# Three-branch attention in one kernel: heads stepped in pairs, other lags, banks and buffers

## The chip, the cores and the metric

The kernel runs on one core of a Trainium2 chip. The core has five engines with instruction queues of their own: TensorE (PE, matrix products; its weight loads are shown as PEld), VectorE (DVE), ScalarE (ACT), GpSimd (POOL) and SyncE (SP, which here only issues DMAs). They share an on-chip memory (SBUF) of 128 partitions, and PE writes its results to eight accumulation banks (PSUM) of 128 x 512 fp32 numbers. The metric is device time in microseconds of the whole program, one launch.

## The reference, cut to what matters

The program is a chain of blocks on 512 tokens of width 1024: a mixer, a cross attention, a gated MLP, a stick-breaking attention, an MLP, the three-branch attention that the change touches, and a last MLP. Of the three-branch attention:

```python
# 16 heads of 64, 4 groups of 4 heads share keys and values; 512 tokens
sc    = einsum(q, k_cmp) * scale            # 31 compressed blocks per group
p_cmp = softmax(where(valid_c, sc, NEG))
o_cmp = einsum(p_cmp, v_cmp)
...
ss    = einsum(q_rot, k_sel) * scale        # 8 blocks of 64: with top 16 of 8, all causal keys
o_sel = einsum(softmax(where(valid_s, ss, NEG)), v_sel)
...
sw    = einsum(q_rot, k_w) * scale          # window of 512: all causal keys again
o_win = einsum(softmax(where(valid_w, sw, NEG)), v_w)
...
out   = einsum(gates, stack([o_cmp, o_sel, o_win]))   # sigmoid gates per token, branch, head
return out @ w_o
```

`q_rot` is the query with a partial rotation. Since the sequence is 512 long, the selected and the window branch are both plain causal attention, each with keys and values of its own; the kernel computes them with the same code, as branch b = 0 and b = 1.

## The kernel before, in words

Every block splits fp32 operands into a high and a low part, and PE multiplies high by high, low by high and high by low. The program is written in a fixed order: each engine executes its instructions in the order in which the Python code emits them, and waits on semaphores where it needs another engine's result. A tile from a pool (`tmp`) with `bufs=n` is reused after n allocations of its tag, and the first writer waits for the last reader of the old content. PSUM banks come from lists by tag (`BANKS`) in rotation, with the same wait.

`n_attend` is the stage in question. It builds a list of steps and loops over them. Each group of four heads has one compressed step (`c_` functions, all four heads at once) and then, for each pair of heads and each branch b, the two heads one after the other, each with four steps: the four chunks of 128 queries in the order `QORD` = 3, 2, 0, 1. Chunk c sees 128(c+1) keys, so its tiles are 512, 384, 128 and 256 wide. That is 33 steps a group and 132 in all. In iteration i, the parts of different steps are emitted with lags, in the order of `ORDER`: the scores of step i (PE, bank `s`), the value products of step i-9 (PE, bank `av`), mask, scaling by -1/8 and row minimum of step i-1 (`n_bias`, DVE, L2065, into a tile `np`), the transpositions of step i-6 (PE, L2087, bank `t`), the exponential with row sum of step i-2 (ACT, L2070), the reciprocal of the sum of step i-3 (DVE, L2074), the scaling by reciprocal and gate of step i-4 (POOL, L2079), the split of a finished pair (`n_head`, ACT L548 and DVE L549), the move of step i-7 from bank `t` into the probability tile `pt` (`n_move`, ACT L2100 for chunks 3 and 0, DVE L2098 for 2 and 1), and last one call of each running generator (`tick`). The value products of a pair and a branch are emitted together once both heads' four chunks are moved: eight products for 64 + 64 output rows, before them, in branch 0, the compressed term.

`g_query(p)` rotates the queries of pair p, in twelve calls: a shuffle on DVE (L2031); six elementwise operations on POOL (L2034, L2036, L2038, twice); then for each of the two heads the high part on ACT (L2044), the low part on DVE (L2046) and a DMA from SP (L2049) that copies both to the other 64 partitions. In the trace each call's instruction stands behind what its engine was given in that iteration. The generator for the next pair starts in step 4 and step 20 of a group and makes one call a step.

Behind the steps, the output projection (`no0` to `no7`) starts with three banks that take the pairs' K blocks (`out(k)`) as they are ready, while the last steps drain.

Of the kernel before, what the change touches and what calls it, by code (L numbers as in the profile page):

```python
# [18 lines left out]
P = 128  # L19
T = 512  # L20
# [11 lines left out]
         "s": [0, 1, 2], "t": [3, 4, 5, 6], "av": [7], "f": [0, 1, 2, 3]}  # L32
NP = 8
# [433 lines left out]
class Kernel:  # L467
# [954 lines left out]
    def fetch(self, upto):  # L1422
        while self.fetched <= min(upto, KT - 1):
            m = self.fetched
            t = self.tmp(self.back_tag[0], bufs=self.back_tag[1])
# [316 lines left out]
    def _nsa(self):  # L1742
# [13 lines left out]
        self.heads = {}  # L1756
# [198 lines left out]
    def gate(self, gt):  # L1955
# [3 lines left out]
        for c in range(4):  # L1959
# [12 lines left out]
    ORDER = (("scores", 0), ("out", 9), ("bias", 1), ("turn", 6), ("exp", 2), ("sums", 3),  # L1972
             ("scale", 4), ("head", 10), ("move", 7), ("tick", 0))
    DRAIN, QSTART = 10, 4

    def n_attend(self):
        self.causal = self.wide("causal", self.ph, "causal")
        steps = []
        for g in range(4):
            steps.append(dict(g=g, c=3))  # L1980
            for h0 in (4 * g, 4 * g + 2):
                for b in range(2):
                    for h in (h0, h0 + 1):
                        for c in self.QORD:
                            steps.append(dict(g=g, h=h, b=b, c=c))
# [10 lines left out]
        for i in range(n + max(lag for _, lag in self.ORDER) + 1):  # L1996
            if i == n:
                lead = [(self.W.get(f"no{m}", 3 - m), self.bank("s")) for m in range(3)]
            for part, lag in self.ORDER:
                if part == "tick":  # L2000
                    self.tick()
                elif 0 <= i - lag < n:
                    u = steps[i - lag]
                    f = getattr(self, ("n_" if "h" in u else "c_") + part, None)
                    if f:
                        f(u)
            if i < n and i % 33 % 16 == self.QSTART and i < 116:
                self.bg.append(self.g_query(i // 33 * 2 + i % 33 // 16 + 1))
            j = i - n - self.DRAIN + 7
            if 0 < j < 8:  # L2010
                out(j - 1)
        nxt, nx = self.next_norm() if self.nxt else None, self.newx() if self.nxt else None
        self.back, self.fetched, self.back_tag = {}, 0, ("np", NP)
# [46 lines left out]
    def n_bias(self, u):  # L2060

        w = P * u["c"] + P
        p = u["p"] = self.tmp("np", bufs=NP)[:, :w]
        u["mx"] = self.tmp("nmx", (P, 1), bufs=8)
# [3 lines left out]
    def n_exp(self, u):  # L2068
        u["sm"] = self.tmp("nsm", (P, 1), bufs=8)
# [3 lines left out]
    def n_sums(self, u):  # L2073
        self.nc.vector.reciprocal(u["sm"], u["sm"])  # L2074
# [15 lines left out]
    def n_move(self, u):  # L2090
        h, b, c = u["h"], u["b"], u["c"]
        if c == self.QORD[0]:
            self.pt[h, b] = self.pt0 if self.npt % 3 == 2 else self.tmp("pt", (P, 13, P), bufs=2)
# [8 lines left out]
    def n_out(self, u):  # L2102
# [5 lines left out]
        if b == 0:  # L2108
            self.av = self.bank("av")
            cp, vc = self.cp  # L2110
            for e in range(2):
                self.mm(self.av[halves[e]], vc[:, (h - 1 + e) % 4, :], cp, True, False)
        pt = [self.pt.pop((h - 1 + e, b)) for e in range(2)]
# [100 lines left out]
```

## Time and profile before

| | |
|---|---|
| median of 3 runs | 2194.77 us (2191.74 to 2198.05) |
| the profiled execution | 2190.76 us |
| its span, first to last instruction | 2187.8 us |
| mean granted TensorE clock | 0.994 of full speed |
| PE busy | 2126.4 us (97%) |
| DVE, ACT, POOL busy | 1218.1, 885.0, 203.2 us |
| scores of the stage, first to last | 1611.57 to 1770.4 us |

Busy time is the time in which an engine had at least one instruction running; matmuls are pipelined, so a busy PE is not PE at its peak. An instruction's start to the next one's start on the same engine is what it occupies, often less than its duration. The stage is about 8% of the span.

### The profile page before, as it was taken

What the parts mean: (1) busy time and instruction counts of PE and PEld (TensorE: products, weight loads), DVE (VectorE), ACT (ScalarE), POOL (GpSimd) and SP (SyncE); (2) the same over time, 40 slices, a digit from 0 to 9 for tenths busy, and PEclk for the clock granted to TensorE, in tenths of its full rate; (3) what the DMA queues carried; (4) which work ended last, traced back from release to release, by engine and by line L of the source; (5) the groups of instructions that cost most, each with busy time, mean ns of one, the idle gap of its engine ahead of it and who ended that gap; (6) DMA issues with size and microseconds to landing.
All of it is one profiled execution on the core that took longest, in us unless ns stands there. A gap on an engine that the chain in (4) does not pass through costs nothing.

```text
span 2187.8 us, 26618 instructions
## 1 busy us (share of the span) xinstructions
PE 2126.4 (97%) x10250; PEld 1728.4 (79%) x10250; DVE 1218.1 (56%) x2052; ACT 885.0 (40%) x1457; POOL 203.2 (9%) x277
## 2 busy tenths in 40 slices
PE   8999999999999999999999999999988899999998
PEld 6788898888888888777688888888766668888886
DVE  5988665654443435566555343456667755534434
ACT  4533543433222224355435232234646744423322
POOL 1000000000000000122100000001047720000000
PEclk9999999999999999999999999999999999999999
DMA  4212444222333323422143233333421023333231
GB/s 148 73 63 78 160 129 135 68 78 87 97 98 97 99 80 110 133 62 75 49 135 97 97 96 97 97 100 123 138 83 31 21 73 102 106 97 98 95 100 64
DMA packets 63375, 205.93 MB, mean 94 GB/s; under 512 B 7952, under 2 KB 8336, under 8 KB 63120
## 3 DMA queue, kind: packets, MB, share of 16 engines
q1 hardware_dynamic: 59504, 196.86, 28.5%
q10 hardware_dynamic: 3744, 7.37, 0.9%
q8 instruction: 80, 1.31, 0.2%
q14 instruction: 47, 0.39, 0.1%
HBM read 189.39 MB, written 6.29 MB: 89 GB/s over the span
## 4 chain that ended last, share of the span: by engine, by line
PE 83%; DVE 7%; ACT 4%; POOL 3%; issue 2%; DMA 1%; ACTq 0%; POOLq 0%; SPq 0%; DVEq 0%
PE psum L539 63%; PE b L539 18%; POOL sph L1680 1%; ACT sT L1662 1%; ACT sT L1663 1%; PE psum L2087 1%; DVE spl L1685 1%; DVE wl L350 1%; DVE np L2065 1%; DVE sT L1657 1%; DMA nq<-nq 1%; DVE t L906 0%; DVE sT L1656 0%; POOL np L2079 0%; DVE st L1608 0%
## 5 line engine op out<-in xcount | busy, mean ns | idle before, releaser
L539 PE MATMUL psum<-xh,wh 128*128 128x512 f32 x1560 | 610.2, 391 | 1.5 <-DVE h L627 0.9
L539 PE MATMUL psum<-xh,wl 128*128 128x512 f32 x1560 | 607.5, 389 | 1.5 <-DVE wl L350 1.4
L539 PE MATMUL psum<-xl,wh 128*128 128x512 f32 x1560 | 607.4, 389 | 0.0
L341 ACT ACTIVATE wh<-ws 128x1024 fp32r<-128x1024 f32 (+1 forms) x346 | 356.9, 1039 | 372.6 <-PE psum L539 315.9
L350 DVE TENSOR_TENSOR wl<-ws,wh 128x1024 fp32r<-128x1024 f32 (+1 forms) x346 | 417.2, 1212 | 97.9 <-ACT wh L341 97.8
L539 PEld LDWEIGHTS psum<-xh,wl 128*128 128x128 f32 x1560 | 292.4, 187 | 64.4 <-DVE wl L350 2.8
L539 PEld LDWEIGHTS psum<-xh,wh 128*128 128x128 f32 x1560 | 292.5, 188 | 63.7 <-issue 2.3
L539 PEld LDWEIGHTS psum<-xl,wh 128*128 128x128 f32 x1560 | 292.5, 188 | 60.3
L539 PE MATMUL b<-xh,wh 128*128 128x512 f32 (+1 forms) x488 | 194.3, 398 | 6.6 <-ACT wh L341 6.6
L539 PE MATMUL b<-xh,wl 128*128 128x512 f32 (+1 forms) x488 | 192.2, 394 | 0.7 <-DVE wl L350 0.7
L539 PE MATMUL b<-xl,wh 128*128 128x512 f32 (+1 forms) x488 | 191.8, 393 | 0.0
L539 PE MATMUL psum<-hh,wh 128*128 128x512 f32 x320 | 125.0, 391 | 0.0
L539 PE MATMUL psum<-hh,wl 128*128 128x512 f32 x320 | 124.6, 389 | 0.0
L539 PE MATMUL psum<-hl,wh 128*128 128x512 f32 x320 | 124.5, 389 | 0.0
L1351 DVE TENSOR_TENSOR h<-h,psum 128x512 f32<-128x512 f32 x48 | 33.0, 688 | 161.2 <-PE psum L539 161.2
L1342 ACT ACTIVATE t<-t 128x512 f32<-128x512 f32 x64 | 40.5, 632 | 188.0 <-DVE t L1341 188.0
L539 PEld LDWEIGHTS b<-xh,wh 128*128 128x128 f32 (+1 forms) x488 | 92.0, 188 | 26.2 <-ACT wh L341 6.8
L539 PEld LDWEIGHTS b<-xh,wl 128*128 128x128 f32 (+1 forms) x488 | 91.7, 188 | 23.4 <-DVE wl L350 2.6
L539 PEld LDWEIGHTS b<-xl,wh 128*128 128x128 f32 (+1 forms) x488 | 92.1, 189 | 19.8 <-DVE xl L552 0.8
L539 PE MATMUL psum<-ks,nq 128*128 128x256 f32 (+2 forms) x256 | 72.5, 376 | 16.4 <-DVE nmx L2065 9.5
L1341 DVE SCALAR_TENSOR_TENSOR t<-psum,r_mlp 128x512 f32<-128x512 f32 x64 | 44.1, 689 | 79.2 <-PE psum L539 79.1
L2079 POOL TENSOR_SCALAR np<-np,nsm,gates 128x512 f32<-128x512 f32 (+3 forms) x128 | 81.2, 640 | 39.8 <-PE psum L2087 17.4
(485 smaller groups left out, 2873.0 us busy)
## 6 DMA issues: line engine op xcount, KB each, us to landing
ws<-in_wst SPq DMA_DIRECT2D x332, 512.0 KB, 3.4
h<-in_xT SPq DMA_DIRECT2D x16, 256.0 KB, 3.7
kk<-kk SPq DMA_DIRECT2D x16, 256.0 KB, 3.6
nq<-nq SPq DMA_DIRECT2D x16, 256.0 KB, 2.9
ws<-in_wst SPq DMA_DIRECT2D x8, 384.0 KB, 3.0
spill<-back SPq DMA_DIRECT2D x8, 256.0 KB, 2.0
back<-spill ACTq DMA_DIRECT2D x8, 256.0 KB, 3.5
spill<-h ACTq DMA_DIRECT2D x8, 256.0 KB, 5.7
```

The lines of the kernel that those rows point to most:

```text
L341: self.nc.scalar.activation(hi[:, :n], s, AF.Copy)
L350: e.tensor_tensor(lo[:, :n], s, hi[:, :n].bitcast(F32), op=ALU.subtract)
L539: self.nc.tensor.matmul(ps, a, b, start=start, stop=stop, skip_group_check=again)
L1341: nc.vector.scalar_tensor_tensor(t, ps, 0.0, norm.bc, op0=ALU.max, op1=ALU.mult)
L1342: nc.scalar.activation(t, t, AF.Square)
L1351: nc.vector.tensor_tensor(self.h[:, m, :], self.h[:, m, :], ps, op=ALU.add)
L1657: self.nc.vector.tensor_scalar(tb, zb[:, :, :384], 30.0, None, op0=ALU.min)
L1662: self.nc.scalar.activation(t, t, AF.Exp)
L1663: self.nc.scalar.activation(t, t, AF.Ln, bias=1.0)
L1680: self.nc.gpsimd.tensor_scalar(hi, t, 1.0, 0.0, op0=ALU.mult, op1=ALU.add)
L1685: self.nc.vector.tensor_tensor(lo, t, hi.bitcast(F32), op=ALU.subtract)
L2079: self.nc.gpsimd.tensor_scalar(u["p"], u["p"], u.pop("sm"), self.gates[:, u["c"], e:e + 1], op0=ALU.mult, op1=ALU.mult)
```

## The change

Both heads of a pair now share a step: a step scores, masks, scales, transposes and moves both heads' chunk c. A group has 17 steps, the stage 68. The lags are new (in steps of two heads): move 5, transpositions 4, value products 6, mask 1, exponential 1, reciprocal 2, scaling 2, split 9, and the move now comes right behind the scores. One reciprocal serves both heads. The value products go into a list of pieces (`todo`: compressed term, key chunk 0, key chunk 1, key chunks 2 and 3), and each step takes one. `tick` makes two calls a step, and the query generators start behind steps 1 and 9 of a group. The `s` tag has four banks instead of three, `t` three instead of four. The masked scores have a tag for each width with 2, 2, 2 and 3 buffers instead of eight shared ones of full width; `pt` has three buffers instead of two (a fourth, `pt0`, lies in another tile). The compressed branch's value tile `vc` is cleared and loaded five steps later and has one buffer. The residual tiles behind the stage are fetched into `pt` buffers, and the first blocks of the output projection are emitted in the seven iterations right behind the last scores.

```diff
 BANKS = {"b": range(8), "bp": [0], "bo": [1], "za": [2, 3], "zb": [4, 6],
-         "s": [0, 1, 2], "t": [3, 4, 5, 6], "av": [7], "f": [0, 1, 2, 3]}
-NP = 8
+         "s": [0, 1, 2, 3], "t": [4, 5, 6], "av": [7], "f": [0, 1, 2, 3]}
+NP = {0: 2, 1: 2, 2: 2, 3: 3}
...
-    ORDER = (("scores", 0), ("out", 9), ("bias", 1), ("turn", 6), ("exp", 2), ("sums", 3),
-             ("scale", 4), ("head", 10), ("move", 7), ("tick", 0))
-    DRAIN, QSTART = 10, 4
+    ORDER = (("scores", 0), ("move", 5), ("turn", 4), ("out", 6), ("av", 0), ("bias", 1),
+             ("exp", 1), ("sums", 2), ("scale", 2), ("head", 9), ("tick", 0))
...
         for g in range(4):
-            steps.append(dict(g=g, c=3))
+            steps.append((dict(g=g, c=3),))
             for h0 in (4 * g, 4 * g + 2):
                 for b in range(2):
-                    for h in (h0, h0 + 1):
-                        for c in self.QORD:
-                            steps.append(dict(g=g, h=h, b=b, c=c))
+                    for c in self.QORD:
+                        two = dict(g=g, h=h0, b=b, c=c), dict(g=g, h=h0 + 1, b=b, c=c)
+                        two[0]["two"] = two[1]["two"] = two
+                        steps.append(two)
...
                 if part == "tick":
-                    self.tick()
+                    self.tick(2)
+                elif part == "av":
+                    if self.todo:
+                        self.todo.popleft()()
                 elif 0 <= i - lag < n:
-                    u = steps[i - lag]
-                    f = getattr(self, ("n_" if "h" in u else "c_") + part, None)
-                    if f:
-                        f(u)
-            if i < n and i % 33 % 16 == self.QSTART and i < 116:
-                self.bg.append(self.g_query(i // 33 * 2 + i % 33 // 16 + 1))
-            j = i - n - self.DRAIN + 7
-            if 0 < j < 8:
-                out(j - 1)
+                    for u in steps[i - lag]:
+                        f = getattr(self, ("n_" if "h" in u else "c_") + part, None)
+                        if f:
+                            f(u)
+            if i % 17 in (1, 9) and i < n - 8:
+                self.bg.append(self.g_query(i // 17 * 2 + i % 17 // 8 + 1))
+            if 0 <= i - n < 7:
+                out(i - n)
...
-        self.back, self.fetched, self.back_tag = {}, 0, ("np", NP)
+        self.back, self.fetched, self.back_tag = {}, 0, ("pt", 3, (P, 13, P))
...
-        p = u["p"] = self.tmp("np", bufs=NP)[:, :w]
-        u["mx"] = self.tmp("nmx", (P, 1), bufs=8)
+        p = u["p"] = self.tmp(f"np{u['c']}", (P, w), bufs=NP[u["c"]])
+        u["mx"] = self.tmp("nmx", (P, 1), bufs=4)
...
     def n_sums(self, u):
-        self.nc.vector.reciprocal(u["sm"], u["sm"])
+        if u["h"] % 2:
+            self.nc.vector.reciprocal(u["sms"], u["sms"])
...
-            self.pt[h, b] = self.pt0 if self.npt % 3 == 2 else self.tmp("pt", (P, 13, P), bufs=2)
+            self.pt[h, b] = self.pt0 if self.npt % 4 == 3 else self.tmp("pt", (P, 13, P), bufs=3)
...
-            cp, vc = self.cp
+        av, (cp, vc) = self.av, self.cp
+        pt = [self.pt.pop((h - 1 + e, b)) for e in range(2)]
+
+        def first():
             for e in range(2):
-                self.mm(self.av[halves[e]], vc[:, (h - 1 + e) % 4, :], cp, True, False)
-        pt = [self.pt.pop((h - 1 + e, b)) for e in range(2)]
-        for j in range(4):
-            for e in range(2):
-                self.mm(self.av[halves[e], P * j:], self.vs[:, b, j, g, :],
-                        pt[e][:, 4 * j:3 * j + 4, :].rearrange("p c q -> p (c q)"),
-                        False, b == 1 and j == 3)
+                self.mm(av[halves[e]], vc[:, (h - 1 + e) % 4, :], cp, True, False)
+
+        def part(js):
+            for j in js:
+                for e in range(2):
+                    self.mm(av[halves[e], P * j:], self.vs[:, b, j, g, :],
+                            pt[e][:, 4 * j:3 * j + 4, :].rearrange("p c q -> p (c q)"),
+                            False, b == 1 and j == 3)
+
+        if b == 0:
+            self.todo.append(first)
+        for js in ((0,), (1,), (2, 3)):
+            self.todo.append(lambda js=js: part(js))
...
     def c_move(self, u):
-        cp = self.tmp("cp", bufs=1)
-        self.nc.scalar.activation(cp, u.pop("ps"), AF.Copy)
-        u["cp"] = cp, u.pop("vc")
+        nc, g = self.nc, u["g"]
+        cp, vc = self.tmp("cp", bufs=1), self.tmp("vc", (P, 4, 64), bufs=1)
+        nc.scalar.activation(cp, u.pop("ps"), AF.Copy)
+        nc.gpsimd.memset(vc, 0.0)
+        for h in range(4):
+            nc.sync.dma_start(out=vc[32 * h:32 * h + 32, h, :],
+                              in_=self.vcs[32 * g:32 * g + 32, :])
+        u["cp"] = cp, vc
```

## Rows read from the trace of the kernel before

**Rows 1.** The page: busy time and share of each engine, instructions.

```profile
PE 2126.4 (97%) x10250; PEld 1728.4 (79%) x10250; DVE 1218.1 (56%) x2052; ACT 885.0 (40%) x1457; POOL 203.2 (9%) x277
```

**Rows 2.** Windows: busy us (count) of PE, PEld, DVE, ACT, POOL, clock, DMA.

```profile
1611.57:1631.14 19.57, 13.68 (x63) 10.19 (x64) 14.93 (x59) 12.93 (x38) 12.80 (x19) 0.83 0.16 40
1631.14:1672.23 41.09, 36.04 (x237) 24.85 (x237) 32.10 (x130) 28.87 (x89) 29.72 (x47) 1.00 0.12 28
...
1754.72:1770.40 15.68, 15.68 (x107) 11.14 (x108) 10.82 (x54) 10.82 (x37) 8.98 (x15) 1.00 0.08 18
1770.40:1788.66 18.26, 17.77 (x97) 12.06 (x95) 6.16 (x17) 4.81 (x14) 3.96 (x6) 1.00 0.23 70
```

**Rows 3.** Chain of waits in the stage: start, us, what.

```profile
1663.50 0.47 PE psum L539 x2
...
1664.88 0.45 PE psum L2087 x4
...
1667.28 1.33 POOL np L2079 x2
...
1669.20 2.89 DMA nq<-nq
1672.23 3.87 PE psum L539 x22
...
1698.94 1.06 POOL np L2172
```

**Rows 4.** Timeline of PE: start us, busy us, line, operation, count.

```profile
1648.84 1.95 PE L539 MATMUL psum<-kb,h 128*128 128x128 f32 x16
1650.72 1.08 PE L539 MATMUL psum<-cp,vc 128*64 128x512 f32 x4
1651.63 0.59 PE L539 MATMUL psum<-pt,vs 128*64 128x512 f32 x1
...
1653.88 0.33 PE L2087 MATMUL psum<-small,np 128*128 128x128 f32 x1
```

**Rows 5.** Timeline of POOL, from the compressed branch's scaling.

```profile
1657.88 1.05 POOL L2172 TENSOR_TENSOR np<-np,csm 128x512 f32<-128x512 f32 x1 [1.55 <-DVE csm L2167]
1658.91 1.41 POOL L2079 TENSOR_SCALAR np<-np,nsm,gates 128x512 f32<-128x512 f32 x2
1660.29 0.73 POOL L2034 TENSOR_TENSOR rsh<-rsh,wd_rope_s 128x256 f32<-128x256 f32 x1
1661.01 0.45 POOL L2079 TENSOR_SCALAR np<-np,nsm,gates 128x128 f32<-128x128 f32 x1
1661.42 0.73 POOL L2036 TENSOR_TENSOR qr<-h,wd_rope_c 128x256 f32<-128x256 f32 x1
```

**Rows 6.** Timeline of all engines, after the last rotation on POOL.

```profile
1667.35 0.63 ACT L2044 ACTIVATE nq<-qr 64x512 fp32r<-64x512 f32 x1
...
1668.01 1.13 DVE L2046 TENSOR_TENSOR nq<-qr,nq 64x512 fp32r<-64x512 f32 x1 [0.46 <-ACT nq L2044]
...
1669.20 2.98 SPq L2049 DMA_DIRECT2D nq<-nq  x2
```

**Rows 7.** Timeline of DVE: move, mask and maximum, in the same group.

```profile
1657.94 0.54 DVE L2098 COPY pt<-psum 128x384 f32<-128x384 f32 x1
1658.40 0.42 DVE L2065 CUSTOM_DVE_ANT_0 np<-psum,wd_causal 128x256 f32<-128x256 f32 x1
...
1660.45 0.55 DVE L2065 CUSTOM_DVE_ANT_0 np<-psum,wd_causal 128x384 f32<-128x384 f32 x1
...
1661.00 0.27 DVE L2065 CUSTOM_DVE_ANT_0 np<-psum,wd_causal 128x128 f32<-128x128 f32 x1
```

**Rows 8.** Windows at the start of the stage, columns as in group 2.

```profile
1612.00:1614.00 2.00, 0.87 (x6) 0.62 (x4) 1.14 (x2) 0.63 (x1) 0.00 (x0) 1.00 0.72 204
...
1616.00:1618.00 2.00, 1.39 (x4) 0.57 (x3) 1.91 (x12) 1.36 (x6) 1.17 (x2) 0.50 0.01 4
1618.00:1620.00 2.00, 2.00 (x11) 2.00 (x11) 1.60 (x10) 1.36 (x4) 2.00 (x4) 0.50 0.00 0
```

More of the change, by code (lines that the diff above doesn't have):

```diff
@@ L1424, in fetch @@
             m = self.fetched
-            t = self.tmp(self.back_tag[0], bufs=self.back_tag[1])
+            tag, bufs, *shape = self.back_tag
+            t = self.tmp(tag, *shape, bufs=bufs)
+            if shape:
+                t = t.rearrange("p n q -> p (n q)")[:, :T]
             self.nc.scalar.dma_start(out=t, in_=self.dram[:, m, :])
@@ L1755, in _nsa @@
         self.gates = ph0.tile([P, 4, 48], F32, name="gates")
-        self.heads = {}
+        self.heads, self.todo = {}, deque()
         self.spill()
@@ L1994, in out @@
                 self.group(ps, w, self.oh, ol, [k], k == 0, k == 7)
-        for i in range(n + max(lag for _, lag in self.ORDER) + 1):
+        for i in range(n + max(lag for _, lag in self.ORDER)):
             if i == n:
@@ L2068, in n_exp @@
     def n_exp(self, u):
-        u["sm"] = self.tmp("nsm", (P, 1), bufs=8)
+        j = u["h"] % 2
+        if j == 0:
+            sm = self.tmp("nsm", (P, 2), bufs=4)
+            for i, v in enumerate(u["two"]):
+                v["sms"], v["sm"] = sm, sm[:, i:i + 1]
         self.nc.scalar.activation(u["p"], u["p"], AF.Exp, bias=u.pop("mx"), scale=-1.0,
@@ L2135, in c_scores @@
                         self.kb[:, g, pr, :], pr == 0, pr == 1)
-        vc = u["vc"] = self.tmp("vc", (P, 4, 64), bufs=2)
-        nc.gpsimd.memset(vc, 0.0)
-        for h in range(4):
-            nc.sync.dma_start(out=vc[32 * h:32 * h + 32, h, :],
-                              in_=self.vcs[32 * g:32 * g + 32, :])
     def c_bias(self, u):
         nc = self.nc
-        p = u["p"] = self.tmp("np", bufs=NP)
+        p = u["p"] = self.tmp("np3", bufs=NP[3])
         mask = self.cst("cmp_mask").rearrange("p (c n) -> p c n", c=4)
```

## The prediction

> **What bounds the kernel now.** The page says that TensorE (PE) is busy 97% of the span [rows 1], but the change touches one stage, so I asked for windows of that stage next. Cut at the waits for a query tile, they show four unlike stretches [rows 2]. In 1754.72 to 1770.40, two heads with both branches and no query being rotated, PE is busy for all of its 15.68 us: this half is PE-bound. A full group (two such halves, a compressed step, two rotations) takes 41.09 us with PE busy 36.04. What would it take if PE were the only limit? Two halves, 31.36, plus the compressed branch's scores, 1.88, and its four transpositions, 0.45 [rows 2 to 4]: 33.7. So some 7.4 us of each group are something else, and no engine is full: DVE 32.1, POOL 29.7, ACT 28.9 of 41.09 [rows 2].
>
> The chain of waits names it. It runs from POOL to PE through a DMA: POOL is in use without a gap from 1657.88 to 1667.28 (the compressed scaling, then scalings and query rotations in turn), then ACT makes the high part of the query, DVE the low part, SP sends it to the other half of the partitions, and PE waits until 1672.23 [rows 3, 5, 6]. From POOL's first scaling to PE's next scores that is 14.35; from there to the next group's compressed scaling (1698.94) it is 26.71 [rows 3, 5]. The wait for both branches' products, which run as one burst (1650.72 to 1653.88, 3.16 us [rows 4]), is PE's own work: it starves the other engines, but costs only where they are the bound.
>
> **The change, part by part.** Matmuls, transpositions, exponentials, moves and scalings keep their number. On PE one head's step of 512 keys is 0.47 for the scores and 0.45 for four transpositions [rows 3]; by columns the four steps make 2.4, four of these per half 9.6, and with products 2 x 2.25 and the compressed term 0.91 [rows 4], 15.0, near the 15.68 measured. PE's floor does not move.
>
> Half of the 128 reciprocals go. A 384-wide mask with its reciprocal takes DVE 0.55 until the next instruction [rows 7]; about 0.08 of it is the reciprocal, so 64 fewer are 5 us of DVE over the stage. DVE has 9 us to spare in each 41 [rows 2]: taken as 0, at most 5 if DVE were full.
>
> Splitting the products into parts gives back nothing in the PE-bound half. In the other halves it may give back the bursts, and no more than the 7.4 per group.
>
> The masked scores' buffers by width (2 or 3 of each instead of 8 shared): a buffer is needed again four steps on, after the transposition of the same width, which PE issues right behind the scores that the mask waits for anyway. I take 0; the upper bound is that of rival 3. One buffer of vc and its four DMAs, five steps later, are read another five steps later, some 10 us against 3 for a DMA: 0. The residual tiles in pt buffers wait for the last products, after which ACT has to split that same result: 0.
>
> The query. Before, a generator's call per single-head step: the rotations spread over six steps, and only the first head's tile was urgent, since the second is read four steps later. Now two calls fall in each step of two heads, so the pace per unit of work is the same, but both heads' tiles are read in the same step, the ninth. I follow it in program order. POOL has between its compressed scaling and the sixth rotation: 1.03, a rotation 0.72, two 512-wide scalings 1.38, two rotations 1.43, two 384-wide 1.2 (between the 0.69 and 0.41 of its neighbours), two rotations 1.43, the clearing of vc (some 0.3), two 128-wide 0.82, the last rotation 0.72: 9.0, against 9.40 before [rows 5]. Behind it: 0.73 until DVE starts the first low part, 1.05 for that; then DVE has, in its order, two moves of 384 (2 x 0.46) and two masks of 384 (1.02 with one reciprocal), and only then the second low part, 1.19 until its DMA is issued, and 3.03 until PE goes on [rows 6, 7]. That is 7.9, where the first tile alone took 4.95. So POOL's compressed scaling to both heads' scores is 17.0 instead of 14.35: **+2.6**.
>
> The transposition banks, 4 before, now 3, two used per step. The second transposition of a step needs the bank that the first head of the step before it used, so its move must be done. In the steps of 512 and 128 keys that move is ACT's. Now ACT's order is the point: the call that makes the first high part stands at the end of the same step as POOL's last rotation, and the move of the 512-wide step is queued behind it. While ACT waits for POOL, PE waits for ACT. In the group's second half: the second head's mask ends 2.3 after its scores start, shuffle, moves and masks of the next step bring DVE to 5.1, POOL's run of 7.1 (no compressed scaling, and it starts with the second rotation) to 12.2, ACT's high part and move to 13.3. PE alone gets there in 10.4 (scores 0.47, transpositions 0.9, steps of 2.3, 1.6, 1.6 and 2.6 with their parts, 1.0 of the next). PE waits 2.9. Then 4.2 of PE work to the compressed scores, and some 7.5 from there to POOL's scaling (9.04 before, without the burst's 3.16, plus the second head's scores, transpositions and mask, 1.6). Sum 25.0 against 26.71: **-1.7**. In the first half the same wait (some 3.5) lies inside the 17.0.
>
> The drain: the seven ready blocks of the output projection now start at once and are used up before the last products, so the last split, 0.63 on ACT and some 0.7 on DVE, stands bare: +1.4. Before, PE had 0.49 idle there [rows 2], and at the cut one head's 0.47 is already done: **+0.4**.
>
> Sum: 2.6 for the first half of the first group, three times 2.6 - 1.7 = 0.9, and 0.4: **+5.7**. The profiled execution took 2190.76 us with a span of 2187.8; the sum makes it 2196.5. The runs' median, 2194.77, stands 0.2% above that execution; carried over it would be 2200.5. I take 2198, between them.
>
> **The rivals.** (1) *Faster: the rotations are covered.* The way from scaling to transposition is two steps of two heads, twice as long as before. If POOL ends its sixth rotation no later than PE reaches the transposition that needs the bank, neither wait occurs. For it: POOL's 29.7 a group fits under PE's 33.7 [rows 2]. Against it: in steps 2 to 5 POOL has 9.0 and PE some 7.4, and POOL starts one to two steps behind. A group would be 33.7 plus some 3 for the second tile, 36.7; three groups save 13, the first half nothing: 2190.8 - 13 = 2178, carried 2180. It decides from a POOL lag under some 3 us. Chance 0.27.
>
> (2) *Slower: PE's clock falls in the new waits.* At the start of the stage PE was busy 0.87 of 2.00 us, and in 1616 to 1620 the granted clock was 0.50, the lower level of 1.2 GHz, with PE busy all of 1618 to 1620 [rows 8]; the idle before 1672.23, shorter, left it at 1.00 [rows 2]. My waits of 2.9 to 3.5 lie between. If each takes the clock down for some 4 us, PE loses 2 us in each half where it is then the bound: two per group, 12 in all, 2209. The Trainium skill (TensorE: Matmul & The Clock Gate, "HAM oscillation — how this bites in real kernels") warns of just this, waits between bursts after which every burst begins at the lower level; by it the time is 2209, by the row of the shorter wait 2198. No row of before has a wait as long inside the steady stage. Chance 0.13.
>
> (3) *Slower: three banks bind in every step.* Where ACT moves (512 and 128 wide), it first ends the exponentials of its step; if PE gets to the second transposition 0.4 earlier, eight such steps a group cost 3.2, the stage 12 more: 2209. For it: PE and ACT are both at some 30 a group. Against: PE has two heads' scores and one head's transpositions to do meanwhile, about 1 us. It decides from there. Chance 0.10.
>
> **How the numbers follow.** My forecast 0.45, the rivals 0.27, 0.13 and 0.10, else 0.05. About 0.3% (6.6 us) is what a measurement of this kernel can tell. The forecast's own range is 2189 to 2207: of its 0.45 some 0.28 are same, 0.15 slower, 0.02 faster. Rival 1 is faster but for 0.02, rivals 2 and 3 slower but for 0.03. With the rest split: faster 0.30, same 0.35, slower 0.35. The range goes from rival 1 to beyond rivals 2 and 3: 2178 to 2212.
>
> **What would show it.** Right: a group of about 42 us; PE waiting some 3 us before a transposition, released by ACT's 512-wide move, with ACT idle until POOL's last rotation; PE waiting for the second query DMA in each group's first half; no burst of products over 1 us. Wrong: groups under 39 us with PE full between query waits (rival 1), a clock under 1.00 inside the groups (2), waits of some 0.4 at every step's second transposition (3).

## The result, and the profile after

The changed kernel takes 2211.48 us (median; 2209.31 to 2212.47) and the kernel before 2193.55 beside it: a ratio of 1.0082, 95% interval 1.0069 to 1.0096, some 18 us slower. The forecast was 2198 within 2178 to 2212: the time lies inside the range, at its upper end, and outside the 2189 to 2207 of the main forecast, so the range was right and the sum behind the forecast was not. The profiled execution took 2211.73 us (span 2209.9).

The page answers [rows 1]: PE's busy time rose by 13.6 us though it runs as many instructions, and DVE has 64 fewer.

```profile
PE 2140.0 (97%) x10250; PEld 1730.0 (78%) x10250; DVE 1214.6 (55%) x1988; ACT 883.7 (40%) x1457; POOL 204.3 (9%) x277
```

Windows of the stage after, cut at the same scores as [rows 2] (columns as there): the first stretch up to the second pair, then three whole groups, the half without a query, and the rest up to the last matmul of the output projection.

```profile
1615.16:1637.46 22.30, 12.88 (x58) 9.33 (x59) 14.60 (x55) 12.33 (x39) 13.61 (x21) 0.84 0.20 48
1637.46:1682.39 44.93, 38.91 (x236) 25.75 (x237) 29.52 (x107) 28.01 (x86) 29.75 (x46) 0.97 0.12 25
1682.39:1726.88 44.49, 39.50 (x235) 25.62 (x236) 30.60 (x113) 28.58 (x88) 29.77 (x46) 0.92 0.12 25
1726.88:1771.04 44.16, 37.85 (x239) 24.56 (x238) 31.04 (x115) 28.29 (x88) 29.87 (x46) 1.00 0.12 26
1771.04:1788.30 17.26, 17.11 (x109) 11.03 (x110) 12.40 (x50) 12.80 (x41) 9.74 (x15) 1.00 0.01 2
1788.30:1844.40 56.10, 53.74 (x248) 39.38 (x247) 26.12 (x41) 18.96 (x31) 3.84 (x6) 1.00 0.32 103
```

And the same last stretch of the kernel before, which the rows ahead of the prediction cut shorter.

```profile
1770.40:1821.98 51.58, 51.09 (x244) 39.65 (x242) 26.37 (x43) 20.19 (x35) 3.96 (x6) 1.00 0.35 113
```

A group took 41.1 to 41.4 before and takes 44.2 to 44.9 now. The half that was PE-bound at 15.68 with no idle is 17.26, with PE busy 17.11: PE's own work grew. The rest of the drain went from 51.58 to 56.10, of which PE's busy time makes 2.65 and its idle 1.87. And in two of three groups the granted clock is under 1.00.

The chain of waits of one group after (start, us, what) answers [rows 3].

```profile
1674.29 0.70 POOL qr L2043
...
1675.55 1.05 ACT pt L2110 x2
...
1678.07 0.61 ACT nq L2049
...
1681.61 0.70 DVE ol L549
...
1682.39 0.57 PE psum L539 x2
...
1694.28 0.70 POOL qr L2043
...
1695.53 0.58 ACT pt L2110
...
1696.25 0.52 PE psum L2097 x3
```

POOL ends its last rotation at 1674.99, ACT makes the high part and only then the 512-wide moves, and PE goes on at 1676.27; in the second half the same at 1694.28 to 1696.25. The query tile's DMA is not in the chain: the step before 1682.39 is the split of the last pair on DVE. The DMA, issued at 1679.4 and 2.9 us on its way, ended at about the same time. The waits over the stage (total us, times, longest) say the same.

```profile
ACT nq L2049 <- POOL qr L2043: 27.6, 7, 4.8
DVE nq L2051 <- ACT nq L2049: 25.8, 7, 5.0
...
PE psum L2097 <- ACT pt L2110: 18.8, 7, 4.5
```

Each of the seven rotations holds ACT, DVE and PE in turn, as forecast. PE's timeline around one of them (start, busy us, line, operation, count) shows the second new thing.

```profile
1676.27 0.52 PE L2097 MATMUL psum<-small,np 128*128 128x128 f32 x3 [3.08 <-ACT pt L2110]
1676.71 0.54 PE L539 MATMUL psum<-pt,vs 128*64 128x384 f32 x1
...
1677.09 0.49 PE L539 MATMUL psum<-pt,vs 128*64 128x384 f32 x1
...
1677.51 0.74 PE L539 MATMUL psum<-ks,nq 128*128 128x256 f32 x4
```

The 384-wide piece starts every 0.38, and 0.42 pass until the scores behind it start. In a burst the same matmuls follow each other in 0.32; this is the version of experiment 9, which has bursts again.

```profile
1705.28 0.49 PE L539 MATMUL psum<-pt,vs 128*64 128x384 f32 x1
...
1705.60 0.49 PE L539 MATMUL psum<-pt,vs 128*64 128x384 f32 x1
...
1705.92 0.38 PE L539 MATMUL psum<-pt,vs 128*64 128x256 f32 x1
```

### The profile page after: what moved, and what is told of

The parts are those of the page before. It is cut to its first block, busy times and chain, and to the rows that moved or that the text cites. A ratio compares the mean times of both kernels' runs of the same rounds, so it can differ in the third digit from the quotient of the medians.

```text
span 2209.9 us, 26583 instructions
## 1 busy us (share of the span) xinstructions
PE 2140.0 (97%) x10250; PEld 1730.0 (78%) x10250; DVE 1214.6 (55%) x1988; ACT 883.7 (40%) x1457; POOL 204.3 (9%) x277
## 4 chain that ended last, share of the span: by engine, by line
PE 83%; DVE 6%; ACT 5%; POOL 3%; issue 2%; DMA 0%; ACTq 0%; POOLq 0%; DVEq 0%; SPq 0%
PE psum L539 62%; PE b L539 18%; POOL sph L1683 1%; PE psum L2097 1%; ACT sT L1665 1%; ACT sT L1666 1%; DVE spl L1688 1%; DVE wl L350 1%; POOL np L2089 1%; DVE sT L1660 1%; ACT np L2079 1%; DVE t L906 0%; DVE sT L1659 0%; DVE st L1611 0%; DVE sT L1673 0%
## 5 line engine op out<-in xcount | busy, mean ns | idle before, releaser
L1341 DVE SCALAR_TENSOR_TENSOR t<-psum,r_mlp 128x512 f32<-128x512 f32 x64 | 44.2, 690 | 79.2 <-PE psum L539 79.1
L1276 DVE TENSOR_TENSOR t<-psum,r_ffn 128x512 f32<-128x512 f32 x44 | 30.3, 691 | 96.9 <-PE psum L539 96.8
```

The lines of the kernel that those rows point to most:

```text
L1276: nc.vector.tensor_tensor(t, ps, norm.bc, op=ALU.mult)
L1341: nc.vector.scalar_tensor_tensor(t, ps, 0.0, norm.bc, op0=ALU.max, op1=ALU.mult)
```

## The experiments

Times are compared with the kernel before on the same chip, by their ratio, since not all runs were on one chip; the interval behind each ratio is 95%. The changed kernel stands at 1.0082, and 0.0010 is 2.2 us. To place a run, this table has the stage's stretches from the PE timeline of each: from one group's compressed scores to the next's, then from the fourth's to the last matmul of the output projection. The last three columns are PE's busy time in the sum, the rest of it (idle), and the mean granted clock.

| kernel | group 1 | group 2 | group 3 | 4 and drain | sum | PE busy | PE idle | clock |
|---|---|---|---|---|---|---|---|---|
| before | 39.85 | 41.07 | 41.43 | 90.64 | 212.99 | 190.63 | 22.36 | 0.98 |
| changed | 44.75 | 43.97 | 44.69 | 98.28 | 231.69 | 201.99 | 29.70 | 0.96 |
| late high part | 48.72 | 47.90 | 47.90 | 101.51 | 246.03 | 212.89 | 33.14 | 0.92 |
| four banks | 45.00 | 44.87 | 43.56 | 97.80 | 231.23 | 206.12 | 25.11 | 0.95 |
| whole products | 44.13 | 45.13 | 47.76 | 98.64 | 235.66 | 205.55 | 30.11 | 0.90 |
| late output blocks | 44.94 | 44.68 | 44.66 | 100.37 | 234.65 | 207.78 | 26.87 | 0.93 |
| early queries | 44.73 | 45.43 | 44.13 | 96.17 | 230.46 | 203.35 | 27.11 | 0.96 |
| early queries, late high part | 47.99 | 44.49 | 44.46 | 98.00 | 234.94 | 203.33 | 31.61 | 0.96 |
| before, early queries | 44.63 | 41.29 | 41.29 | 88.43 | 215.64 | 192.93 | 22.71 | 0.97 |
| before, four score banks | 39.53 | 40.69 | 44.06 | 92.13 | 216.41 | 193.27 | 23.14 | 0.96 |
| before, split products | 40.75 | 41.17 | 41.80 | 94.92 | 218.64 | 200.13 | 18.51 | 0.98 |
| before, early queries, later splits | 44.30 | 42.98 | 41.63 | 91.65 | 220.56 | 196.38 | 24.18 | 0.96 |
| combined | 43.15 | 41.94 | 43.63 | 94.43 | 223.15 | 193.57 | 29.58 | 0.96 |
| combined, heads in turn | 41.48 | 39.30 | 39.32 | 95.72 | 215.82 | 194.32 | 21.50 | 0.95 |

**1. The high part a step later.**

```diff
+        yield
         for j in range(2):
             q = self.ph0.tile([P, 2, T], F32R, ...)
```

> The changed kernel, with the query generator giving up one call between the last rotation and the first high part, so that ACT makes it a step later, behind the 512-wide move and not ahead of it. If ACT's wait for POOL is what holds PE (my forecast's wait): the seven waits of PE for an ACT move, 18.8 us in all, nearly go. In the second halves of a group what follows is PE's own work, so three times 1.6 us are gained; in the first halves the wait comes back at the next scores, since the tile comes no earlier. Sum -5: 2206 us. If PE's own work in small pieces is the loss: no change, 2211. If the query tile is what PE really waits for: the delay of the tile is paid, +1 us in each of seven halves at most: 2214 to 2218.

2226.44 us, 1.0137 (1.0123 to 1.0151): 12 us slower than the changed kernel by the ratios, where my theory had 5 faster. From the timeline of all engines:

```profile
1681.47 0.92 DVE L2052 TENSOR_TENSOR nq<-qr,nq 64x512 fp32r<-64x512 f32 x1 [4.24 <-ACT nq L2050]
...
1683.00 0.30 PE L2098 MATMUL psum<-small,np 128*128 128x128 f32 x1 [2.10 <-DVE pt L2109]
...
1689.59 0.70 PE L539 MATMUL psum<-ks,nq 128*128 128x512 f32 x2 [1.88 <-DMA nq<-nq]
```

The same blockade has moved one queue on. ACT no longer stands ahead of its move, but DVE stands 4.24 us at the low part until ACT has made the late high part; DVE's 384-wide move is queued behind, and PE waits 2.10 for it. Then the tile itself is late: 1.88 at the scores. In either queue the moves of two heads stand behind the call. But these waits are the smaller part of the loss. In the table PE's idle time grew by 3.4 us against the changed kernel and its busy time by 10.9, at a mean granted clock of 0.92 against 0.96. One of its groups (columns as in [rows 2]):

```profile
1662.66:1710.56 47.90, 41.34 (x238) 27.05 (x236) 30.55 (x115) 28.98 (x90) 28.73 (x47) 0.93 0.11 24
```

So most of this run's loss goes with the lower clock behind its waits, not with the waits themselves.

**2. Four banks for transpositions, three for scores.**

```diff
-"s": [0, 1, 2, 3], "t": [4, 5, 6]
+"s": [0, 1, 2], "t": [3, 4, 5, 6]
...
-(("scores", 0), ("move", 5), ("turn", 4), ("out", 6), ("av", 0), ("bias", 1), ...
+(("bias", 1), ("scores", 0), ("move", 5), ("turn", 4), ("out", 6), ("av", 0), ...
```

> The changed kernel with three banks for scores and four for transpositions; so that three are enough for the scores, a step's masks are issued ahead of the next step's scores, not behind its transpositions. If three transposition banks are the price (PE stands at the second transposition of a step until the move of the step before is done): PE's 18.8 us behind ACT's moves go, a step of some 2 us later the same bank is needed again, so at most 1.6 us a second half stay away: -5, 2206. If the loss is PE's work in small pieces or the query tile: 2210 to 2212, and the waits only change their name.

2208.95 us, 1.0063 (1.0049 to 1.0076): by the ratios 4 us less than the changed kernel, with intervals that overlap, so the run does not decide between the two cases. PE's waits for ACT moves went from 18.8 us to none, and this line took their place in the view of PE's waits:

```profile
PE psum L539 <- DVE nmx L2070: 22.4, 21, 2.8
```

**3. Whole products.**

```diff
-        for js in ((0,), (1,), (2, 3)):
+        for js in ((0, 1, 2, 3),):
```

> The changed kernel with the products of a pair and branch in one burst again, at the step at which their first part stands now. If the loss is PE's switching between short pieces (0.35 us per pair and branch over 16, and the compressed term's): -5 to -6, 2205 to 2206, and the PE-bound half at the end of the stage, 17.26 now, goes to about 15.9. If waits behind ACT and POOL are the loss: no gain, 2211, since the burst only moves idle time, or slower by up to the 0.5 us by which it holds up the next masks, eight times: 2215.

2213.95 us, 1.0084 (1.0070 to 1.0098): no gain. But the windows of its second and third group, with the clock, forbid to read this as "pieces cost nothing":

```profile
1654.79:1699.92 45.13, 38.31 (x238) 27.04 (x237) 30.76 (x114) 28.45 (x90) 29.80 (x47) 0.92 0.11 25
1699.92:1747.68 47.76, 41.29 (x239) 28.68 (x237) 30.95 (x114) 28.55 (x90) 29.89 (x47) 0.86 0.13 28
```

The clock is 0.92 and 0.86 (PE idle 6.8 and 6.5), so what PE may save in pieces is covered by the lower level. The run is inconclusive for the pieces alone; experiment 7 measures them almost without this (mean clock 0.98), and experiment 8 has whole products in a group at full clock.

**4. Output blocks three steps later.**

```diff
-            if 0 <= i - n < 7:
-                out(i - n)
+            if 3 <= i - n < 10:
+                out(i - n - 3)
```
(and the loop one step longer)

> The changed kernel with the output projection's ready blocks three steps later, as far behind the last scores as in the kernel before, and one more step of the loop for it. The drain took 73.4 us against 67.3. If the missing cover for the last head's split (0.9 us of waiting) and the cuts between blocks and product pieces (some 0.1 to 0.3 us each, seven times) are its price: -2 to -4, 2207 to 2209. If the blocks now fill waits for moves and scalings, as they come early: those waits come back, and the time stays at 2210 to 2213.

2212.01 us, 1.0071 (1.0059 to 1.0084): within the interval of the changed kernel. Its last stretch takes 100.37 us against 98.28, at a clock of 0.98 against 1.00, so it shows no gain there. The waits of 0.70 and 0.22 for the last split are gone; in exchange a wait of 1.89 for an ACT move stands where the blocks had filled in (the 1.43 above it was there before, as 1.44), in PE's timeline:

```profile
1788.29 0.95 PE L2097 MATMUL psum<-small,np 128*128 128x128 f32 x7 [1.43 <-DVE pt L2108]
1791.13 0.52 PE L2097 MATMUL psum<-small,np 128*128 128x128 f32 x3 [1.89 <-ACT pt L2110]
```

**5. Early queries in the changed kernel, and with the late high part.**

```diff
-            if i % 17 in (1, 9) and i < n - 8:
-                self.bg.append(self.g_query(i // 17 * 2 + i % 17 // 8 + 1))
+            if i == 1:
+                self.bg.append(self.g_query(1))
+            if i % 17 in (5, 13) and i < 50:
+                self.bg.append(self.g_query(i // 17 * 2 + i % 17 // 8 + 2))
```

> The changed kernel with every query rotation but the first started four steps earlier (calls in steps 14 to 0 and 6 to 9 of a group's 17), so that the tile is ready four steps before its scores and POOL's last rotation no longer falls behind the compressed scaling. ACT's high part still stands ahead of the move of its step. If the way from POOL through ACT, DVE and the DMA to the scores is the loss: three times the 2.6 of the first halves and the waits at the scores (some 1.2 each) go, and with less idle time the lower clock, which the runs so far show for 17 to 48 us of the stage: 2195 to 2200. If ACT's call ahead of the move is the loss by itself: PE's waits for ACT moves stay near 18 us and the time at 2208 to 2212. If PE's own work is: 2210.

2209.90 us, 1.0073 (1.0061 to 1.0086). Waits for the tile are gone inside the groups, PE's waits for ACT moves stay at 17.7 us, as the second case had it. Its groups 2 and 3 take 45.43 and 44.13 us, against 43.97 and 44.69. So the way of the query to its scores is not what the changed kernel loses.

> The same early start, and the generator gives up one call between the last rotation and the first high part, which alone made the changed kernel 15 us slower. With the tile four steps early this delay costs nothing, so the two edits part what the delay did: if ACT's call ahead of the 512-wide move holds PE, 5 us below the early start alone (2190 to 2195), with PE's waits for ACT moves near 0. If the delay was slow for another reason than the tile's lateness (its place in DVE's and ACT's order), it is slower than the early start again, by up to 15 us.

2212.74 us, 1.0089 (1.0074 to 1.0105): the delay costs nothing of the 12 us of experiment 1 now that the tile is early, but gains nothing either (the intervals overlap); in the stage PE waits 12.4 for DVE's moves and 9.1 for ACT's in place of 17.7 for ACT's. Its two steady groups ran at full clock, which makes them the cleanest measure of PE's own work (windows, columns as in [rows 2]):

```profile
1659.12:1703.61 44.49, 38.30 (x238) 24.66 (x236) 31.52 (x114) 28.65 (x88) 28.73 (x47) 1.00 0.12 25
1703.61:1748.07 44.46, 38.27 (x238) 24.64 (x236) 31.53 (x114) 28.64 (x88) 28.72 (x47) 1.00 0.12 26
```

PE is busy 38.3 a group, against 36.04 at the same clock in [rows 2]. Without the lower clock of experiment 1 the late high part shows no loss; that the waits there took the clock down fits this, but no run holds the clock fixed.

**6. Early queries, and the banks, in the kernel before.** The first:

```diff
-            if i < n and i % 33 % 16 == self.QSTART and i < 116:
-                self.bg.append(self.g_query(i // 33 * 2 + i % 33 // 16 + 1))
+            if i == 4:
+                self.bg.append(self.g_query(1))
+            if i % 33 in (10, 26) and i < 100:
+                self.bg.append(self.g_query(i // 33 * 2 + i % 33 // 16 + 2))
```

> The kernel before with its query rotations started ten single-head steps earlier, nothing else. Its chain of waits ran through POOL, ACT, DVE and the DMA to the scores in each first half, 14.35 us; PE had 7.4 us in each group that were not its own work. If that chain bounds the kernel before: 3 to 5 us per group go, three times, 2180 to 2186. If the bursts of products bound it: no change, 2195.

2194.24 us, 1.0002 (0.9993 to 1.0011). The DMA waits of the steady groups (3.2 us in two groups) are gone, and the groups still take 41.29. The ratio near 1 is a sum of unlike parts, as the table shows: the first group, in which two rotations now overlap, lost 4.8 us, and the last stretch gained 2.2; the two steady groups carry the reading. PE's waits in these two groups:

```profile
PE psum L539 <- DVE nmx L2067: 6.2, 14, 0.8
PE psum L2089 <- POOL np L2081: 3.0, 8, 0.5
```

The second:

```diff
-"s": [0, 1, 2], "t": [3, 4, 5, 6]
+"s": [0, 1, 2, 3], "t": [4, 5, 6]
```

> The kernel before with the changed kernel's split of the banks alone: four for scores, three for transpositions. If three transposition banks cost by themselves (an ACT or DVE move that holds PE): +0.3 to +1 us a group and the drain nothing, 2196 to 2200, with waits of PE for moves that the kernel before has none of. If the banks only bind because two heads share a step: no change, 2194; if the fourth score bank takes away the waits for masks, the 9.5 us of them over 18: 2188 to 2192.

2194.11 us, 1.0001 (0.9991 to 1.0012): the banks alone cost and give nothing.

**7. Split products in the kernel before.**

```diff
+        def part(js):
+            if b == 0 and js[0] == 0:
+                ...
+        for js in ((0,), (1,), (2, 3)):
+            self.todo.append(lambda js=js: part(js))
...
-("head", 10)
+("av", 0), ("head", 11)
...
-    DRAIN, QSTART = 10, 4
+    DRAIN, QSTART = 11, 4
```

> The kernel before with the products in three parts in successive single-head steps (the compressed term with the first part), and the last split of a pair and the blocks of the output projection one step later with it. If short pieces cost PE by themselves, as the two groups at full clock say (PE busy 38.3 against 36.0 a group, both masks and scores alike): +2.3 in each of three groups, +1.6 in the half at the end and some in the first: +6 to +9, 2200 to 2203. If the pieces give back the wait that a burst makes, as the change has it: 2190 to 2194.

2199.24 us, 1.0034 (1.0022 to 1.0046), some 7.5 us slower. A window of one group:

```profile
1653.31:1694.48 41.17, 37.73 (x238) 23.67 (x237) 31.81 (x130) 28.67 (x90) 29.72 (x46) 1.00 0.13 28
```

PE's busy time rises from 36.03 to 37.73 in a group, yet the group stays at 41.2: there the pieces fill idle time. Over the whole stage PE's busy time rose by 9.5 us and its idle time fell by 3.9. The pieces are paid where PE is the bound, in the last stretch, 94.92 against 90.64 in the table; up to 1.8 of these 4.3 us are the clock, which was short by as much there, and the output blocks came a step later in this version too.

**8. Four edits together.** Experiments 2, 3, 4 and 5 (without the late high part) in one kernel.

```diff
+"s": [0, 1, 2], "t": [3, 4, 5, 6]
...
+(("bias", 1), ("scores", 0), ("move", 5), ("turn", 4), ...
...
+            if i % 17 in (5, 13) and i < 50:
...
+            if 3 <= i - n < 10:
...
+        for js in ((0, 1, 2, 3),):
```

> The changed kernel with whole products, four transposition banks (masks first), the early queries and the later blocks of the output projection, all four at once. Each alone left the time within 2 us of the changed kernel, in the whole-product run with the lower clock for 48 us of the stage. If they were each hidden by the next wait: 2193 to 2200, PE busy 36 a group. If two heads in one step are the loss whatever stands around them: 2207 to 2212, with waits for masks and a clock under 1.00.

2202.90 us, 1.0043 (1.0030 to 1.0055): between the two cases. By the ratios the edits gave 4.2, -0.4, 2.4 and 2.0 us alone, 8.2 in sum, and 8.6 of the 18 together. Each of these numbers is uncertain by some 4 us, so that one repair hid another is not shown. A group at full clock:

```profile
1652.49:1694.43 41.94, 35.80 (x238) 25.06 (x237) 30.93 (x113) 28.24 (x90) 30.10 (x47) 1.00 0.12 27
```

PE's work is back at the level of before (35.8); what is left is idle, 6.1 us (5.0 in the kernel before), all of it put down to masks on DVE.

**9. The same, heads in turn.** All parts of the first head in a step, then all of the second; one generator call and one reciprocal for each head (so the 64 saved reciprocals are given up too), and the products with the second head.

```diff
-            for part, lag in self.ORDER:
+            for e in range(2):
+                for part, lag in self.ORDER:
...
-                    for u in steps[i - lag]:
+                        for u in steps[i - lag][e:e + 1]:
```

> The combined version (whole products, four transposition banks, early queries, later output blocks), but within each step all parts of the first head are issued before those of the second, one generator call and one reciprocal for each head; lags in work, buffers and banks stay. If it is two heads' scores, moves, masks and scalings in a row that make the waits left over (24.4 us for masks): 2193 to 2197, the level of the kernel before. If buffers by width and the lag of four steps make them: no change, 2201 to 2204.

2193.50 us, 1.0004 (0.9995 to 1.0013): the level of the kernel before, as the first case had it. Its second and third group:

```profile
1650.99:1690.29 39.30, 35.61 (x238) 24.97 (x237) 31.27 (x130) 28.89 (x89) 30.04 (x47) 1.00 0.13 29
1690.29:1729.61 39.32, 35.63 (x239) 24.99 (x238) 31.27 (x130) 28.91 (x89) 30.05 (x47) 1.00 0.13 29
```

39.3 us a group, 2.6 and 4.3 less than the combined version (whose third group ran at a clock of 0.96), and less than the 41.1 and 41.4 of the kernel before, with much the same busy time on every engine. But its first group takes 41.48 against 39.85 and its last stretch, at a clock of 0.96, 95.72 against 90.64, which eats all of that. The timeline of all engines there:

```profile
1766.81 1.21 DVE L350 TENSOR_TENSOR wl<-ws,wh 128x1024 fp32r<-128x1024 f32 x1
...
1768.58 1.51 DVE L350 TENSOR_TENSOR wl<-ws,wh 128x1024 fp32r<-128x1024 f32 x1 [0.57 <-ACT wh L341]
...
1770.92 1.61 PE L2099 MATMUL psum<-small,np 128*128 128x128 f32 x6 [2.65 <-DVE nsm L2086]
```

DVE makes low parts of output weights ahead of the last masks, and PE waits 2.65 us for a reciprocal behind them; in 1768 to 1790 the granted clock is 0.84. A version that takes these weights two steps later was not tried; whether it beats both kernels stays open.

**10. The kernel before with early queries and later splits.** The low part of a pair's result holds DVE 19.3 us over the stage in the kernel before; this puts it two steps later, the last pair's apart.

```diff
-("scale", 4), ("head", 10), ("move", 7), ("tick", 0)
+("scale", 4), ("head", 12), ("last", 10), ("move", 7), ("tick", 0)
```
(with `n_last` for the last pair, a loop of the same length, and the early queries of experiment 6)

> The kernel before with the early queries (which alone changed nothing) and the split of a pair's result two single-head steps later, but for the last pair. In the trace of before DVE stands 19.3 us, eight times, at the low part of that split, until ACT has made the high part, which waits 14.2 us for the products. If that wait in DVE's order, and not the query, paces a group (41.2 whatever the query does): one to two us in each of eight halves go, 2182 to 2188. If the group is paced by the engines' loads with a rotation among them: no change, 2193.

2197.99 us, 1.0030 (1.0019 to 1.0041): slower, where I expected a gain or nothing. With early queries alone DVE waited in two steady groups 6.0 us at the split and 8.1 at masks; here the first is gone and the second is

```profile
DVE np L2067 <- PE psum L539: 10.1, 5, 3.3
```

A wait in DVE's order that PE does not see is no gain when it goes. Why it became slower I have not found. The granted clock may be part of it: the means of its seven executions are 0.990 to 0.994, where 12 of the 16 of the kernel before beside it have 0.994; but its one execution at 0.994 took 2197.99 us as well.

## Why the prediction was right and wrong

**The waits: right in kind.** ACT's call of the high part ahead of the 512-wide move, with PE held at the second transposition, was forecast at some 3.5 us in the first halves and 2.9 in the second. PE stands 4.50 in the first group's first half and 3.08 in the three others, and 1.57 to 1.76 in the second halves, seven waits in all. POOL's run from the compressed scaling to the second tile's scores took 16.67 (forecast 17.0). The first half of the first group took 24.75 against 22.15, the +2.6 forecast; with a wait of 4.50 and a clock of 0.50 behind it, neither of which is in the sum, this agreement is in part luck. And as a price the waits were wrong: other waits went as these came. PE's idle time in groups 2 and 3 was 5.04 and 5.32 before and is 6.35 and 4.96 now. This is the whole stage in the kernel before, the changed one, the combined one and the one with the heads in turn:

```profile
1608.99:1821.98 212.99, 190.63 (x1138) 137.40 (x1137) 150.01 (x542) 130.69 (x373) 115.15 (x178) 0.98 0.18 50
1612.71:1844.40 231.69, 201.99 (x1138) 137.50 (x1138) 145.87 (x478) 129.19 (x373) 116.58 (x178) 0.96 0.17 46
1609.34:1832.49 223.15, 193.57 (x1137) 140.30 (x1137) 145.55 (x478) 128.74 (x373) 117.23 (x178) 0.96 0.18 48
1609.51:1825.33 215.82, 194.32 (x1137) 140.93 (x1137) 147.75 (x542) 131.15 (x373) 116.41 (x178) 0.95 0.18 49
```

Of the 18.7 us that the change added (forecast 5.7), 11.4 are PE's busy time, up to 5 of them the lower clock, and 7.3 are idle, 3.8 of it in the first group and 2.6 in the last stretch.

**"PE's floor does not move": the step that failed.** I counted columns, and of the split I asked only what it gives back ("nothing in the PE-bound half"), not what it takes. My sum by columns, 15.0, had even come out 0.7 under the 15.68 measured, and I left that unexplained. A pair's products in one branch take 1.01 + 0.80 + 0.80 in pieces and 0.91 + 0.64 + 0.75 in a burst, some 0.3 more, and in the changed kernel's order PE's group is 38.3 instead of 36.0 at full clock (experiment 5). With whole products, and the three other edits of experiment 8, it is 35.8 with the heads still in pairs. The split alone costs the kernel before 7.5 us.

**The second half, -1.7: wrong in sign.** The three groups took 10.0 us more, not 2.7. Of the sum for the second half, 13.3 to the transposition became 13.86, 4.2 to the compressed scores 5.18, 7.5 to POOL's scaling 8.3: 27.3, above the 26.71 of before. Most of the excess lies in the last two, in which PE is busy nearly throughout: I had taken them at the old pace.

**The drain, +0.4: mis-sized.** It took 73.4 from the middle of the last group, against 67.3: +6.1. 1.6 are in the PE-bound half, where PE's busy time grew by 1.4; in the rest 2.65 are PE's work (pieces between output blocks) and 1.87 idle, of which the bare split that I had counted is 0.92 and a wait of 1.44 behind weight splits on DVE I had not. Experiment 4 moves the blocks back, and the last stretch gets no shorter.

**The premise that the query's chain bounds a group: wrong.** I read it from the chain of waits. Experiments 6 and 5 start the rotations early, the tile's waits go, and neither kernel's steady groups get shorter. The chain names who released PE last; with that released earlier, masks and scalings are as late. What the change costs beside PE's own work is, as far as shown, the order of issue: two heads' moves, masks and scalings in a row on queues that work in order. Putting the heads in turn took 8.6 us off (1.0043 to 1.0004, intervals apart) with all lags in work, banks and buffers as they were. A reciprocal and a generator call for each head came with it and were not tried apart, nor was the order tried on the changed kernel without the four edits.

So of some 18 us, four edits together account for half and the order of the heads for the other. The stage's lines above part the two: with the four edits PE's busy time goes from 201.99 to 193.57 and its idle time stays (29.7 and 29.6), at the same clock; with the heads in turn the busy time stays and the idle time goes to 21.5. The whole products are the edit that changes PE's own work, so they are likely most of the first half; alone (experiment 3) they show no gain, at a clock of 0.90, so this division is argued and not shown. Nor are the same losses all gone: the last stretch is still 5 us longer than before, and the steady groups are shorter.

**The rivals.** The faster one did not occur: the rotations were not covered. The clock rival (0.13) occurred behind two of the seven waits, not behind each:

```profile
1674.00:1676.00 2.00, 0.00 (x0) 0.00 (x0) 0.33 (x1) 0.99 (x2) 2.00 (x4) 1.00 0.05 11
1676.00:1678.00 2.00, 1.73 (x11) 0.99 (x12) 2.00 (x6) 2.00 (x6) 0.06 (x1) 1.00 0.18 41
1678.00:1680.00 2.00, 2.00 (x19) 1.43 (x17) 1.76 (x8) 1.95 (x7) 1.27 (x1) 1.00 0.45 96
...
1718.00:1720.00 2.00, 0.00 (x0) 0.00 (x0) 0.37 (x1) 1.03 (x3) 2.00 (x4) 0.76 0.06 12
1720.00:1722.00 2.00, 1.78 (x7) 0.80 (x7) 1.81 (x4) 1.98 (x7) 0.01 (x1) 0.50 0.18 42
1722.00:1724.00 2.00, 2.00 (x8) 1.25 (x6) 1.50 (x7) 1.95 (x6) 1.04 (x1) 0.50 0.44 94
```

Both stretches hold the end of a PE wait of 3.08 us for an ACT move (the PE timeline above, and again at 1720.22). Through the first the granted clock stays at 1.00; in the second it falls before the wait ends and is 0.50, the 1.2 GHz level, for some seven us. The third wait of 3.08, at 1764.92, left it at 1.00, and the one of 4.50, at 1631.17, was followed by 0.50 until past 1640. The group with the drop at 1720 took 44.69 and the one without 43.97, 0.7 us, where the rival priced a drop at 2. Over the stage the clock was short by 8.5 us of full speed against 3.5 before, so it explains at most 5 of the 18 in this execution. The Trainium skill (TensorE: Matmul & The Clock Gate, "HAM oscillation — how this bites in real kernels") tells of a kernel in which the burst after every wait for a DMA began at the lower level; here the bursts after one of the three waits of 3.08 us and after the one of 4.50 did. Three banks in every step, the last rival, is excluded: the waits for ACT's moves come only with the rotations, and with four banks they are gone, waits for masks have come in their place, and the time fell by 4 us, within the uncertainty.

**The range.** That 2211.48 fell inside 2178 to 2212 is luck. The upper end was set by two rivals of 2209 each. One did not occur and the other occurred in part; the time came there by PE's own work and by idle at the two ends of the stage, which had no such price in the prediction.

## What to carry to other kernels

A chain of waits names the last releaser, not the bound: move it earlier by itself, in the old kernel too, before pricing a change by it. When work of two units is issued side by side, write out each engine's order: a call that waits stands ahead of both units' moves, and putting it later only hands the wait to the next queue. Price a burst cut into pieces from the start-to-start times at its edges, and look for it in the stretch where that engine is the bound; elsewhere it fills idle time. And before you read a run as a verdict on its edit, split its stretch into PE's busy time, PE's idle time and the granted clock: waits that come can replace waits that go, and a longer busy time can be the clock.

## What the runs showed of the hardware that I had not expected

The lower clock has no fixed price. Over 1600 to 1850 the granted clock, summed from windows of 10 us, was short by 3.5 us of full speed in the kernel before, 8.5 in the changed one and 24.1 with whole products. In the changed kernel a drop of 3.4 us of full speed made a group 0.7 us longer. In the kernel before with the other banks (experiment 6) one made it 3.4 us longer, with PE as long idle as without:

```profile
1652.01:1692.70 40.69, 35.73 (x238) 25.18 (x237) 32.05 (x130) 28.96 (x89) 29.67 (x47) 1.00 0.13 28
1692.70:1736.76 44.06, 39.08 (x238) 26.07 (x237) 32.08 (x130) 28.96 (x89) 29.69 (x47) 0.92 0.12 26
```

Whole executions differ in the same way. Two of the changed kernel with mean clocks of 0.992 and 0.988, 8.8 us apart by that, took 2211.73 and 2212.47 us; three of the kernel with the other banks at 0.994 took 2188.80 to 2191.28, and six at 0.991 took 2193.91 to 2196.91. And waits of equal length, 3.08 us, in the same place of three groups were followed by different clocks, so a kernel with waits of this size cannot be priced by their length alone.
